# A second mixer whose scores use half of the matrix array each, and PSUM banks that are handed out in pairs

## The chip, the cores and the metric

The kernel runs on one core of one Trainium2 chip. A core has five engines that run side by side and wait for each other on counters: PE (TensorE, matrix products from SBUF into PSUM), DVE (VectorE), ACT (ScalarE), POOL (GpSimd) and SP, which issues transfers. Each engine works through its own list of instructions in the order in which the program gives them, so an instruction that waits holds up everything behind it on its engine. PSUM, into which PE writes, is used here as eight banks of 128 partitions by 512 fp32 numbers.

The metric is the device time of one execution in microseconds (us), the median over several runs.

## The reference: what is computed

Two layers on x of 256 tokens by 1024. Each layer is a half-weighted SwiGLU feed-forward part (hidden width 2816), a token mixer, and a second feed-forward part, all with RMSNorm in front and a residual around. The first layer's mixer is a gated DeltaNet; the second layer's mixer, which the change is about, is sliding-window attention:

```
proj = h @ w_in + b_in                      # 16 query heads, 4 key and value heads, 64 wide
s = einsum("bnqhgd,bnkhd->bnhgqk", q, kk) * 64**-0.5     # kk: this block of 128 keys and the one before
s = where(band of 128 keys, s, -inf)
p = softmax(concat([s, sink]))[..., :-1]
y = (p @ vv) @ w_out + b_out
```

There are two blocks of 128 tokens. Block 0 sees its own keys, block 1 sees its own and those of block 0.

## The kernel before, in words

Everything is resident in SBUF except the weights, which stream in once, 177 MB in all. Each 512 KB piece of weights (`raw`) is split in two fp32r parts: ACT rounds it to `whi` (line 296) and DVE subtracts to get `wlo` (line 297). A product then is two or three matrix products, such as `whi` by the high and low part of the activations side by side (line 348, 512 columns) and `wlo` by the high part (line 349, 256 columns).

**Feed-forward part** (`ffn`). After a first chunk that is done in another way, ten chunks of 256 hidden columns follow. A chunk makes four PSUM tiles, two of the gate (`pg`) and two of the up half (`pu`); each tile takes 16 matmuls, eight at line 348 and eight at line 349. Then the tile is emptied: ACT copies one half of it to SBUF (line 424 for a gate, 433 for an up tile) and DVE adds the other half to the copy (line 425 or 434). ACT's SiLU, POOL's product and the split of the result follow from SBUF. The down projection then accumulates in four or five `acc` tiles.

**Second mixer** (`swa`). The keys were written into `kz`, which holds each key head twice, in rows 0 to 63 for the one and rows 64 to 127 for the other head of a pair, with zeros elsewhere (POOL writes the zeros at line 1106). So one matmul with all 128 rows gives the scores of two query heads (`score`, line 1152): three of them for a pair of heads `j`, for block 1 against the older keys (`psp`) and for both blocks against their own (`psc`). DVE picks by mask (line 1162), adds the causal mask (1163) and takes the maximum (1166); ACT takes four exponentials out of PSUM (1176); POOL scales; PE transposes (`ppt`, 1186) and multiplies by the values (`po`, 1196).

**PSUM.** Two tags, `psA` and `psB`, have four buffers of one bank each. A new tile of a tag takes a buffer when everything that touched the tile in it is over.

**Order.** Nobody wrote the order of the engines' lists by hand, apart from a few `issue_after` edges. The framework collects the instructions and their dependences by tile, and a planner with an estimate of each duration orders every engine's list and hands out the buffers. So a change of the PSUM tiles may move instructions anywhere in the program.

Of the kernel before, what the change touches and what calls it, by code (L numbers as in the profile page):

```python
# [9 lines left out]
F32 = mybir.dt.float32  # L10
F32R = mybir.dt.float32r
AF = mybir.ActivationFunctionType
# [3 lines left out]
P = 128  # L16
D = 1024
T = 256
NT = T // P
# [9 lines left out]
BKV = 4  # L29
# [6 lines left out]
class Ticker:  # L36
    def __init__(self):
        self.active = []
# [167 lines left out]
class Kern:  # L206
    def __init__(self, ctx, tc):
        self.tc = tc
        self.nc = tc.nc
        self.cp = ctx.enter_context(tc.tile_pool(name="const", bufs=1))  # L210
        self.wp = ctx.enter_context(tc.tile_pool(name="wts", bufs=5))
        self.bp = ctx.enter_context(tc.tile_pool(name="big", bufs=11))
        self.sp = ctx.enter_context(tc.tile_pool(name="small", bufs=2))
        self.pp = ctx.enter_context(
            tc.tile_pool(name="ps", bufs=4, space=bass.MemoryType.PSUM)
        )
        self.consts()
        self.hold = None

# [881 lines left out]
    def swa(self, nrm, prep, w_in, w_out, after):  # L1101
        nc = self.nc
        bcol, bv, sk, bo = prep
        NP = BH // 2
        kz = self.big([P, BKV, 2, T], "kz")
        nc.gpsimd.memset(kz, 0.0)
        qT = self.big([P, NP, T], "qT")
        v = self.c2([P, NT, BKV * HD], "v")
        tk = Ticker()
# [18 lines left out]
        for f in range(2):  # L1128
            ps = self.psA("pk")
            self.proj_T(ps[:, :T], w, f, nrm)  # L1130
            for i in range(2):
                src = slice(64 * i, 64 * i + 64)
                for half in range(2):
                    dst = slice(64 * half, 64 * half + 64)
                    if half == i:
                        nc.scalar.activation(kz[dst, 2 * f + i, half, :], ps[src, :T], AF.Identity,
                                             bias=bcol[src, 8 + f:9 + f])
                    else:
                        nc.vector.tensor_scalar(kz[dst, 2 * f + i, half, :], ps[src, :T],
                                                bcol[src, 8 + f:9 + f], None, op0=ALU.add)  # L1140
        oT_h = self.big([P, KT, T], "oTh", F32R)
        oT_l = self.big([P, KT, T], "oTl", F32R)
# [1 line left out]
        def attend(j):  # L1144
            kv = j // 2
# [5 lines left out]
            def score(out, b, kt):  # L1151
                nc.tensor.matmul(out, lhsT=qT[:, j, b * P:(b + 1) * P], rhs=kz[:, kv, :, kt * P:(kt + 1) * P],  # L1152
                                 start=True, stop=True)
# [8 lines left out]
            nc.vector.copy_predicated(sc[:, 1], self.gt.bitcast(mybir.dt.int32).unsqueeze(1).to_broadcast([P, 2, P]), sp)  # L1162
# [11 lines left out]
            for b in range(NT):  # L1174
# [6 lines left out]
                out=pr, in0=pr, in1=l.unsqueeze(3).to_broadcast([P, NT, 2, P]), op=ALU.mult)  # L1181
            yield
            yield
            ps = self.psA("ppt")
            for n in range(4):
                nc.tensor.transpose(ps[:, n * P:(n + 1) * P], prv[:, n, :], self.ident)
            pv = ps.rearrange("p (b h q) -> p b h q", b=NT, h=2)
# [1 line left out]
            nc.vector.tensor_tensor(out=pT[:, 1:3], in0=pv[:, 1:2].to_broadcast([P, 2, 2, P]),  # L1189
                                    in1=self.M["st"].unsqueeze(2).to_broadcast([P, 2, 2, P]), op=ALU.mult)  # L1190
            yield
            po = self.psA("po")
            for b in range(NT):
                for i in range(2):
                    for kt in range(b + 1):
                        lastpo[0] = nc.tensor.matmul(po[64 * i:64 * i + 64, b * P:(b + 1) * P],  # L1196
                                         lhsT=v[:, kt, kv * HD:(kv + 1) * HD], rhs=pT[:, b + kt, i, :],
                                         start=kt == 0, stop=kt == b)
# [129 lines left out]
```

## Time and profile before

| | before |
|---|---|
| median of 3 runs (lowest, highest) | 1031.75 us (1031.38, 1031.99) |
| the profiled execution's own time | 1030.34 us |
| its span in the profile | 1028.6 us |
| PE busy | 1003.0 us, 98% of the span |
| DVE, ACT, POOL busy | 649.5, 552.5, 244.8 us |
| data moved | 177.05 MB, 172 GB/s on the mean |

A row of the timeline gives the start in us, the duration in us, engine, line, operation, output and inputs, shapes, and in square brackets how long the engine stood idle before and what ended that. A row of the windows view gives a stretch, its length, then for each engine the busy time and the number of instructions, then the granted clock of PE, the share of the transfer engines and GB/s. PE is drawn busy until a product has left its pipeline, so the starts of two matmuls that follow each other, and not their ends, tell how long one holds the array.

### The profile page before, as it was taken

To read this page: it belongs to the slowest core of one execution; us is meant where nothing else is said; L and a number is where in the kernel's file an instruction comes from. 1 tells how busy PE (TensorE), PEld (TensorE's weight loads), DVE (VectorE), ACT (ScalarE), POOL (GpSimd) and SP (SyncE) were. 2 spreads that over 40 slices of the span, in tenths; PEclk is the share of its full clock that TensorE was granted. 3 is DMA by queue.
4 is the path that set the end of the run, shared out by engine and by line. 5 is a ranking of instruction groups with operands and counts; after the bars stand their busy time and mean duration, and the time that the engine had idled before them with its cause. 6 is when DMAs were issued, how large, how long until landed. Compare 5 with 4: busy or idle time off the path is not lost.

```text
span 1028.6 us, 16500 instructions
## 1 busy us (share of the span) xinstructions
PE 1003.0 (98%) x6211; PEld 873.3 (85%) x6211; DVE 649.5 (63%) x967; ACT 552.5 (54%) x1007; POOL 244.8 (24%) x277
## 2 busy tenths in 40 slices
PE   8999999999979999999999999999999999999997
PEld 6888888899878888888888888888898678888886
DVE  6866654666896766666645666664567756666544
ACT  7556543457755646555434555554366645555432
POOL 2233610006744201322200032330021401323100
PEclk9999999999989999999999999999999999999999
DMA  7666666644443335666665666666653426666661
GB/s 250 202 190 186 192 198 196 187 149 127 129 150 90 122 104 164 194 187 193 198 192 182 189 200 187 184 204 193 203 188 120 136 90 205 195 188 192 200 189 42
DMA packets 135252, 177.05 MB, mean 172 GB/s; under 512 B 7186, under 2 KB 120196, under 8 KB 135172
## 3 DMA queue, kind: packets, MB, share of 16 engines
q1 hardware_dynamic: 131968, 171.46, 54.9%
q10 hardware_dynamic: 3204, 4.53, 1.5%
q8 instruction: 49, 0.80, 0.3%
q14 instruction: 31, 0.25, 0.1%
HBM read 174.92 MB, written 1.05 MB: 171 GB/s over the span
## 4 chain that ended last, share of the span: by engine, by line
PE 62%; issue 1%; DVE 1%; ACT 1%; POOLq 0%; POOL 0%; ACTq 0%
PE pg L348 11%; PE pu L348 11%; PE acc L343 7%; PE acc L341 7%; PE acc L342 7%; PE pu L349 6%; PE pg L349 6%; PE pgu L343 1%; PE pgu L342 1%; PE pgu L341 1%; PE pq L341 1%; PE pq L343 1%; PE pq L342 1%; PE psc L1152 1%; PE po L1196 1%
## 5 line engine op out<-in xcount | busy, mean ns | idle before, releaser
L297 DVE TENSOR_TENSOR wlo<-raw,whi 128x1024 fp32r<-128x1024 f32 x302 | 379.9, 1260 | 202.7 <-ACT whi L296 201.7
L296 ACT CAST whi<-raw 128x1024 fp32r<-128x1024 f32 x316 | 330.3, 1052 | 184.8 <-PE acc L343 84.2
L348 PE MATMUL pg<-hs,whi 128*128 128x512 f32 x640 | 225.6, 394 | 0.3 <-DVE hs L203 0.3
L348 PE MATMUL pu<-hs,whi 128*128 128x512 f32 x640 | 225.1, 393 | 0.0
L349 PE MATMUL pu<-hs,wlo 128*128 128x256 f32 x640 | 179.7, 281 | 0.3 <-DVE wlo L297 0.3
L349 PE MATMUL pg<-hs,wlo 128*128 128x256 f32 x640 | 178.9, 280 | 0.0
L348 PEld LDWEIGHTS pg<-hs,whi 128*128 128x128 f32 x640 | 119.9, 187 | 27.7 <-DVE hs L203 0.7
L348 PEld LDWEIGHTS pu<-hs,whi 128*128 128x128 f32 x640 | 119.8, 187 | 27.0
L435 POOL TENSOR_TENSOR act<-act,gate 128x256 f32<-128x256 f32 x80 | 60.2, 752 | 346.5 <-DVE act L434 337.7
L342 PE MATMUL acc<-wlo,ah 128*128 128x512 f32 (+1 forms) x340 | 128.4, 378 | 0.0
L343 PE MATMUL acc<-whi,al 128*128 128x512 f32 (+1 forms) x340 | 128.2, 377 | 0.0
L341 PE MATMUL acc<-whi,ah 128*128 128x512 f32 (+1 forms) x340 | 127.8, 378 | 0.0
L349 PEld LDWEIGHTS pu<-hs,wlo 128*128 128x128 f32 x640 | 120.9, 189 | 0.6 <-DVE wlo L297 0.6
L349 PEld LDWEIGHTS pg<-hs,wlo 128*128 128x128 f32 x640 | 120.9, 189 | 0.4
L341 PEld LDWEIGHTS acc<-whi,ah 128*128 128x128 f32 x340 | 64.0, 188 | 12.0
L342 PEld LDWEIGHTS acc<-wlo,ah 128*128 128x128 f32 x340 | 64.0, 188 | 11.8
L343 PEld LDWEIGHTS acc<-whi,al 128*128 128x128 f32 x340 | 63.9, 188 | 11.9
L438 POOL TENSOR_SCALAR ah<-act 128x256 fp32r<-128x256 f32 x80 | 69.0, 862 | 6.8
L341 PE MATMUL pcv<-hs,whi 128*128 128x256 f32 x192 | 56.5, 294 | 5.9 <-DVE cv L883 5.9
L424 ACT COPY gate<-pg 128x256 f32<-128x256 f32 x80 | 29.5, 369 | 58.9 <-PE pg L349 58.9
L433 ACT COPY act<-pu 128x256 f32<-128x256 f32 x80 | 29.5, 369 | 55.9 <-PE pu L349 55.9
L94 POOL TENSOR_TENSOR rst<-var,mhalf 128x1 f32<-128x1 f32 x10 | 5.6, 557 | 213.7 <-DVE var L92 213.7
(340 smaller groups left out, 1555.7 us busy)
## 6 DMA issues: line engine op xcount, KB each, us to landing
raw<-in_ffn_w_gu_dram SPq DMA_DIRECT2D x160, 512.0 KB, 4.4
raw<-in_ffn_w_down_dram SPq DMA_DIRECT2D x88, 512.0 KB, 4.2
raw<-in_a_w_in_dram SPq DMA_DIRECT2D x32, 512.0 KB, 4.5
raw<-in_ffn_w_gu_dram SPq DMA_DIRECT2D x32, 256.0 KB, 4.7
raw<-in_b_w_in_dram SPq DMA_DIRECT2D x12, 512.0 KB, 4.9
raw<-in_a_w_out_dram SPq DMA_DIRECT2D x8, 512.0 KB, 3.7
raw<-in_b_w_out_dram SPq DMA_DIRECT2D x8, 512.0 KB, 3.7
nw<-in_ffn_norm_dram ACTq DMA_DIRECT2D x3, 512.0 KB, 4.3
```

Of the source, the lines that this page charges most:

```text
L296: nc.scalar.copy(hi, raw)
L297: (eng or nc.vector).tensor_tensor(out=lo, in0=raw, in1=hi.bitcast(F32), op=ALU.subtract)
L341: nc.tensor.matmul(out, lhsT=lh, rhs=rh, start=start, stop=False)
L342: nc.tensor.matmul(out, lhsT=lh, rhs=rl, start=False, stop=False)
L343: return nc.tensor.matmul(out, lhsT=ll, rhs=rh, start=False, stop=stop)
L348: nc.tensor.matmul(out, lhsT=lh, rhs=r2, start=start, stop=False)
L349: return nc.tensor.matmul(out[:, :T], lhsT=ll, rhs=rh, start=False, stop=stop)
L424: nc.scalar.copy(g, pg[:, T:])
L433: nc.scalar.copy(a, pu[:, T:])
L435: nc.gpsimd.tensor_tensor(out=a, in0=a, in1=gates[f], op=ALU.mult)
L438: ahead[2] = nc.gpsimd.tensor_scalar(oh, a, 1.0, None, op0=ALU.mult)
L1152: nc.tensor.matmul(out, lhsT=qT[:, j, b * P:(b + 1) * P], rhs=kz[:, kv, :, kt * P:(kt + 1) * P], start=True, stop=True)
```

## The change

Three things are edited. In `swa`, the keys `kk` are kept once per half of the partitions, without zeros, and the scores of each head of a pair are computed by matmuls over its own 64 rows: four in place of three for a pair of heads, two with 256 columns and two with 128. The two heads' results lie in two different banks, so a pair of banks is taken as one tile (`pair`, two buffers of two banks each). `psA` now hands out the two halves of such a pair in turn, for every user of `psA` in the whole kernel, the feed-forward parts and the first mixer among them. And `ppt` and `po` move from `psA` to `psB`.

```diff
+        self.half = None
...
+    def pair(self, name):
+        self.half = None
+        return self.pp.tile([P, 2, 512], F32, tag="psA", name=name, bufs=2)
+
     def psA(self, name):
-        return self.pp.tile([P, 512], F32, tag="psA", name=name)
+        if self.half is None:
+            pair = self.pair(name)
+            self.half = pair[:, 1]
+            return pair[:, 0]
+        half, self.half = self.half, None
+        return half
...
-        kz = self.big([P, BKV, 2, T], "kz")
-        nc.gpsimd.memset(kz, 0.0)
+        kk = self.big([P, BKV, T], "kk")
...
-                        nc.scalar.activation(kz[dst, 2 * f + i, half, :], ps[src, :T], AF.Identity,
+                        nc.scalar.activation(kk[dst, 2 * f + i, :], ps[src, :T], AF.Identity,
...
-            psc, psp = self.psB("psc"), self.psB("psp")
-            sc = psc.rearrange("p (b h k) -> p b h k", b=NT, h=2)
-            sp = psp[:, 0:256].rearrange("p (h k) -> p h k", h=2)
-            score(sp, 1, 0)
-            score(sc[:, 1], 1, 1)
-            score(sc[:, 0], 0, 0)
+            ps = self.pair("psc")
+            for c, b, n in ((128, 1, 2), (0, 0, 1)):
+                for i in range(2):
+                    hs = slice(64 * i, 64 * i + 64)
+                    nc.tensor.matmul(ps[:, i, c:c + n * P], lhsT=qT[hs, j, b * P:(b + 1) * P], rhs=kk[hs, kv, 0:n * P],
+                                     start=True, stop=True)
+            sc = ps.rearrange("p h (b k) -> p b h k", k=256)[:, :, :, 0:P]
...
-            ps = self.psA("ppt")
+            ps = self.psB("ppt")
...
-            po = self.psA("po")
+            po = self.psB("po")
```

**How the order moves.** In the changed program line numbers are up to 14 higher (348, 349, 296, 297, 424 and 425 are now 360, 361, 308, 309, 436 and 437). Numbers behind names tell buffers apart; both halves of a pair bear the name that the first one got.

PE in the middle of the first feed-forward part, the first matmul of each tile (the 15 others of a tile are left out), before:

```order
L348 MATMUL pg_632<-hs_88,whi_620 128x512
...
L348 MATMUL pg_653<-hs_88,whi_620 128x512 [waits DVE_49]
...
L348 MATMUL pu_686<-hs_88,whi_674 128x512 [waits DVE_49]
...
L348 MATMUL pu_709<-hs_88,whi_674 128x512 [waits DVE_49]
...
L348 MATMUL pg_744<-hs_88,whi_732 128x512 [waits DVE_49]
```

and of the change:

```order
L360 MATMUL pu_567<-hs_88,whi_555 128x512 [waits DVE_49]
...
L360 MATMUL pu_677<-hs_88,whi_665 128x512 [waits DVE_49]
...
L360 MATMUL pg_624<-hs_88,whi_612 128x512 [waits DVE_49]
...
L360 MATMUL pg_734<-hs_88,whi_722 128x512 [waits DVE_49]
...
L360 MATMUL pu_677<-hs_88,whi_665 128x512 [waits DVE_49]
```

Before, the two tiles of a gate follow each other and then the two of an up half. Now halves of two pairs alternate: second half of `pu_567`, first of `pu_677`, second of `pg_624`, first of `pg_734`, second of `pu_677`. The counter value that a first half waits for is, in the built program, that of the DVE add which empties the half written directly before it: `pg_734` takes over the two banks of `pg_624` and waits for the add on the second half of `pg_624`, the tile right ahead of it in PE's list. A second half waits for the add on the first half of its own pair. Before, `pg_744` takes over the bank of `pg_632`, the fourth tile before it.

ACT's and DVE's lists of the change around the same place, with the emptying of the second half of `pg_624` (`gate_661`):

```order
L308 CAST whi_728<-raw_730 128x1024 [waits DMAHW6_49,PE_49,Activation_49]
L308 CAST whi_775<-raw_777 128x1024 [waits DMAHW7_49,PE_49,Activation_49]
L436 COPY gate_661<-pg_624 128x256 [waits PE_49,Pool_49]
L445 COPY act_694<-pu_677 128x256 [waits Pool_49]
L438 ACTIVATE gate_661<-gate_661 128x256 [waits DVE_49]
```

```order
L309 TENSOR_TENSOR wlo_729<-raw_730,whi_728 128x1024 [waits DMAHW6_49,PE_49,Activation_49]
L309 TENSOR_TENSOR wlo_776<-raw_777,whi_775 128x1024 [waits DVE_49,DMAHW7_49,PE_49,Activation_49]
L437 TENSOR_TENSOR gate_661<-gate_661,pg_624 128x256 [waits Activation_49]
L446 TENSOR_TENSOR act_694<-act_694,pu_677 128x256 [waits DVE_49,Activation_49]
L451 TENSOR_TENSOR al_131<-act_694,ah_128 128x256 [waits Pool_49]
```

The rows ahead of the copy and of the add are as they were before: two casts ahead of the one, two subtractions ahead of the other. The second cast waits, by its PE count, for the last line-360 matmul of that very tile, whose `whi` buffer it overwrites.

PE at the scores of the second and third pair of heads, of the change:

```order
L1167 MATMUL psc_7764<-kk_7462,qT_7463 128x256 [waits DVE_49,PE_49,Activation_49]
L1167 MATMUL psc_7764<-kk_7462,qT_7463 128x256
L1167 MATMUL psc_7764<-kk_7462,qT_7463 128x128 x2
...
L1167 MATMUL psc_7832<-kk_7462,qT_7463 128x256 [waits Activation_49]
L1167 MATMUL psc_7832<-kk_7462,qT_7463 128x256
L1167 MATMUL psc_7832<-kk_7462,qT_7463 128x128 x2
```

Where three full-height matmuls stood for a pair of heads, four of 64 rows stand now, and `psc_7764` waits for the last exponential that reads the scores before it.

More of the change, by code (lines that the diff above doesn't have):

```diff
@@ L1135, in swa @@
                     if half == i:
-                        nc.scalar.activation(kz[dst, 2 * f + i, half, :], ps[src, :T], AF.Identity,
+                        nc.scalar.activation(kk[dst, 2 * f + i, :], ps[src, :T], AF.Identity,
                                              bias=bcol[src, 8 + f:9 + f])
                     else:
-                        nc.vector.tensor_scalar(kz[dst, 2 * f + i, half, :], ps[src, :T],
+                        nc.vector.tensor_scalar(kk[dst, 2 * f + i, :], ps[src, :T],
                                                 bcol[src, 8 + f:9 + f], None, op0=ALU.add)
@@ L1149, in attend @@
             prv = pr.rearrange("p b h k -> p (b h) k")
-            def score(out, b, kt):
-                nc.tensor.matmul(out, lhsT=qT[:, j, b * P:(b + 1) * P], rhs=kz[:, kv, :, kt * P:(kt + 1) * P],
-                                 start=True, stop=True)
-            psc, psp = self.psB("psc"), self.psB("psp")
-            sc = psc.rearrange("p (b h k) -> p b h k", b=NT, h=2)
-            sp = psp[:, 0:256].rearrange("p (h k) -> p h k", h=2)
-            score(sp, 1, 0)
-            score(sc[:, 1], 1, 1)
-            score(sc[:, 0], 0, 0)
-            nc.vector.copy_predicated(sc[:, 1], self.gt.bitcast(mybir.dt.int32).unsqueeze(1).to_broadcast([P, 2, P]), sp)
+            ps = self.pair("psc")
[5 more added lines that the diff above has]
+            sc = ps.rearrange("p h (b k) -> p b h k", k=256)[:, :, :, 0:P]
+            nc.vector.copy_predicated(sc[:, 1], self.gt.bitcast(mybir.dt.int32).unsqueeze(1).to_broadcast([P, 2, P]),
+                                      ps[:, :, P:2 * P])
             nc.vector.tensor_tensor(out=sc[:, 0], in0=sc[:, 0], in1=self.neg.unsqueeze(1).to_broadcast([P, 2, P]),
```

## The prediction

> **What bounds the kernel now.** I read the page's busy shares first, then its clock strip and the shares of the chain of waits.
>
> ```profile
> span 1028.6 us, 16500 instructions
> PE 1003.0 (98%) x6211; PEld 873.3 (85%) x6211; DVE 649.5 (63%) x967; ACT 552.5 (54%) x1007; POOL 244.8 (24%) x277
> PEclk9999999999989999999999999999999999999999
> PE 62%; issue 1%; DVE 1%; ACT 1%; POOLq 0%; POOL 0%; ACTq 0%
> ```
>
> PE is busy in 98% of the span, at full clock in all but one of forty slices; DVE (63%) and ACT (54%) have room, and the chain runs through PE. So whatever makes PE wait lengthens the end by its whole length. Next I read the timeline of the first feed-forward part around the end of a gate tile.
>
> ```profile
> 475.66 0.39 PE L348 MATMUL pg<-hs,whi 128*128 128x512 f32 x1
> 475.89 0.28 PE L349 MATMUL pg<-hs,wlo 128*128 128x256 f32 x1
> 476.01 0.39 PE L348 MATMUL pu<-hs,whi 128*128 128x512 f32 x1
> 476.13 1.05 ACT L296 CAST whi<-raw 128x1024 fp32r<-128x1024 f32 x1 [0.34 <-PE pg L348]
> ...
> 477.08 0.37 ACT L424 COPY gate<-pg 128x256 f32<-128x256 f32 x1
> 477.21 1.23 DVE L297 TENSOR_TENSOR wlo<-raw,whi 128x1024 fp32r<-128x1024 f32 x1 [0.16 <-ACT whi L296]
> ...
> 478.36 0.42 DVE L425 TENSOR_TENSOR gate<-gate,pg 128x256 f32<-128x256 f32 x1
> ```
>
> The gate tile's last matmul starts at 475.89 and the next tile has the array from 476.01, without a gap. The tile is empty only when the add ends, at 478.36 + 0.42 = 478.78, 2.77 us later. Nobody feels it: four buffers stand in a ring, and the next tile into that bank comes three tiles on. The windows view of two tiles gives their length:
>
> ```profile
> 470.46:476.01 5.55, 5.55 (x35) 4.89 (x34) 3.88 (x7) 3.14 (x5) 1.66 (x3) 1.00 0.64 195
> ```
>
> 5.55 us for two tiles, PE busy throughout, clock 1.00. Emptying (2.77) is as long as one tile (5.55 / 2 = 2.78), and has three tiles of cover.
>
> **Term 1, the pairs.** The edit turns four separate banks into two pairs, and the order of the changed program shows what that does: a pair's first half waits for the add on the second half of the pair whose banks it takes, which is the tile PE has just written (`pg_734` behind `pg_624`). A second half waits for the add on the first half of its own pair, one tile further back, although that lies in another bank: two tiles of cover there, so no cost. So the cover of every other tile falls from three tiles to none. In the built order such a wait on the tile directly ahead stands at 17 places in each of the four feed-forward parts, 68 in all; the program before has none in these loops.
>
> Its price: ACT's and DVE's rows ahead of copy and add are the same as before, and the last cast ahead of the copy still waits for that tile's last line-348 product. So the chain above applies: cast 1.05 (released 0.12 us after the slot 476.01), copy behind it, subtraction to 478.44, add to 478.78. For the step from a DVE result to PE's restart I take the nearest restart of this kind:
>
> ```profile
> 814.76 0.34 DVE oTl L1201
> 815.15 0.73 PE L343 MATMUL acc<-whi,oTl 128*128 128x512 f32 x2 [1.64 <-DVE oTl L1201]
> ```
>
> 0.05 us (815.15 less 815.10). A stall is 2.77 + 0.05 = 2.82 us; everything behind on PE stands too, since its list is strict. Bounds: nothing shorter than copy and add alone, 0.37 + 0.42 with hand-overs of 0.12 (476.01 to 476.13), 0.03 (cast end 477.18 to 477.21) and 0.05, together 1.0 us, if casts and subtractions ran early; nothing above 3.3 if a second cast of 1.05 is only half done when the tile ends. I take 2.82, since the queue order that gave it stands unchanged. **68 x 2.82 = 192 us.**
>
> **Term 2, the clock.** PE's granted clock is not constant once PE pauses. Slices of 3.41 us around three pauses, and matmuls inside a slow one:
>
> ```profile
> 273.55:276.96 3.41, 2.16 (x19) 1.95 (x17) 3.33 (x5) 0.57 (x2) 2.86 (x3) 1.00 0.11 16
> 276.96:280.38 3.42, 3.25 (x27) 3.26 (x28) 3.39 (x4) 3.42 (x9) 2.29 (x1) 1.00 0.86 296
> 290.62:294.03 3.41, 0.49 (x5) 0.28 (x3) 3.41 (x4) 0.00 (x0) 1.89 (x2) 0.99 0.23 61
> 294.03:297.44 3.41, 0.48 (x2) 0.51 (x3) 3.41 (x8) 0.42 (x1) 0.00 (x0) 0.50 0.87 291
> 355.47:358.88 3.41, 1.86 (x10) 1.25 (x9) 1.87 (x8) 2.17 (x12) 1.61 (x2) 1.00 1.04 350
> 358.88:362.30 3.42, 2.80 (x25) 2.57 (x24) 1.73 (x7) 1.50 (x8) 0.41 (x1) 1.00 0.28 97
> 812.85:816.26 3.41, 1.76 (x9) 0.68 (x7) 3.24 (x10) 2.83 (x11) 1.03 (x2) 1.00 0.87 285
> 816.26:819.68 3.42, 3.40 (x16) 2.77 (x17) 2.54 (x3) 1.67 (x4) 2.31 (x2) 0.50 0.90 270
> 297.31 0.42 PE L342 MATMUL pcv<-hs,whi 128*128 128x256 f32 x1
> 297.53 0.42 PE L343 MATMUL pcv<-hs,wlo 128*128 128x256 f32 x1
> ```
>
> The two drops to 0.50 lie on one grid of 3.413 us (812.85 - 290.62 = 153 steps), and so I cut the others. A slice with 1.76 us or less of PE work is followed by a whole slice at 0.50, one with 1.86 or 2.16 by full clock. At 0.50 matmuls of 256 columns follow each other every 0.22 us (297.31 to 297.53) where they take 0.12 at full clock (475.89 to 476.01). So with idle time above about 1.65 us in one slice the next one does half its work. A stall of 2.82 us can hide from that only if a grid line cuts it so that neither side exceeds 1.65, that is between 1.17 and 1.65 us into it: 0.48 of 3.41, 14% of placements. In 52% it lies with all its idle time plus a whole busy slice behind it, losing 3.41 / 2 = 1.71 us; in 34% the slow slice holds the stall's tail and loses about 1.4. Mean 0.52 x 1.71 + 0.34 x 1.41 = 1.37; the top is 1.71. Since stalls follow each other every two tiles, a slow slice makes the next tiles longer and moves the phase; I take 1.5. **68 x 1.5 = 102 us**, between 0 (no rule as I read it) and 116.
>
> The Trainium skill speaks against this term: "TensorE: Matmul & The Clock Gate", Part 1, has the clock fall after an idle window of about 3.4 us; by that rule no stall of 2.82 us costs clock and the sum would be about 1238. The trace disagrees once: 1.65 us of idle time in the slice from 812.85 were enough.
>
> **Term 3, ends of the feed-forward parts.** The first products of the down projection wait for casts that stand behind the last gate tile's emptying; by the same chain, 1.5 us in each of four parts (0 to 3): **+6** (0 to 12).
>
> **Term 4, the first mixer.** Its `pcv` tiles come out of `psA` too:
>
> ```profile
> L883 DVE SCALAR_TENSOR_TENSOR cv<-pcv,wc,cv 128x253 f32<-128x253 f32 (+2 forms) x72 | 32.5, 472 | 10.9 <-ACT cv L880 10.4
> L880 ACT ACTIVATE cv<-pcv,wc 128x256 f32<-128x256 f32 x24 | 11.2, 472 | 5.1 <-PE pcv L343 5.0
> ```
>
> Emptying takes one ACT and three DVE instructions, 4 x 0.47 = 1.9 us. In the new order six such waits have 0.2 to 1.7 us of PE work ahead; they fall short by some 4.2 us together, and by up to 18 with a cast and a subtraction ahead. **+6** (0 to 20).
>
> **Term 5, the second mixer.**
>
> ```profile
> 780.32 0.43 PE psp L1152 x2
> 780.75 0.86 PE psc L1152 x4
> 782.18 0.37 ACT L1176 ACTIVATE att<-psc,smx 128x128 f32<-128x128 f32 x1
> 783.23 0.37 ACT L1176 ACTIVATE att<-psc,smx 128x128 f32<-128x128 f32 x1
> 787.21 0.59 PE po L1196 x8
> 787.81 0.59 PE ppt L1186 x4
> L1106 POOL MEMSET kz<- x1: 1813/1813/1813, 744.3 to 744.3; 128x2048 f32 x1
> ```
>
> The chain of waits gives 0.43 us for each of three score products per pair of heads: 8 x 3 x 0.43 = 10.3 us in all. The columns are the same now (2 x 256 + 2 x 128 against 3 x 256), so the gain is 0 if two 64-row products go one after the other, and half, 5.2, if they overlap. The trace has no 64-row product; the nearest, 64-column `po`, takes 0.074 each (0.59 / 8) where full-size transposes take 0.15 (0.59 / 4) on fewer columns, which says that narrow products are not dearer. I take the middle, **-2.6**.
>
> The Trainium skill's "TensorEngine Tiling (Array Packing)", Key Properties, lets two 64-row tiles work at once but drains PE at a change of mode; by its full gain the sum would be 2.6 us lower. No run shown so far has such products.
>
> Against it, a score pair is held from its first product (780.32) to its last exponential (783.23 + 0.37), about 3.3 us, or 4.3 with a cast ahead, while 24 projection products of 0.12 (2.9 us) stand between. Four places, 0.5 to 2.8 us each: **+5** (0 to 11). The memset (1.81 us) leaves POOL, which is idle three quarters of the span, and its row names nobody who waited for it: 0. `ppt` and `po` in `psB` find as many buffers as before: 0.
>
> **Sum.** 192 + 102 + 6 + 6 + 2.4 = 308 us. On the profiled execution's own time, 1030.34 (span 1028.6), that is 1339; the median, 1031.75, is 0.14% higher, which gives **1340**.
>
> **The rivals.**
>
> *The clock stays up* (0.10). For it: slices with 1.55 us of idle time (355.47) kept full clock, and only two drops are seen. Against it: 812.85. It would be 1031.75 + 192 + 14 = 1238.
>
> *Casts run early* (0.04). With PE stopped, casts and subtractions of later pieces could be done, leaving copy and add: 68 x 1.0 = 68 us, and a stall of 1.0 us leaves every slice over 1.86 us of work, so no half clock: 1031.75 + 68 + 14 = 1114. Against it: the cast ahead of the copy needs that tile's own last products.
>
> *Two slow slices for each stall* (0.05). If a slow slice with part of a stall in it counts as idle again, a second one follows: 68 x 1.5 more, about 1440.
>
> *The stalls are not there, and the change is faster* (0.02). One mechanism: the wait of a pair's first half stands one add earlier than I read it, on the tile before the last. Then emptying (2.77) ends as that wait comes up (a tile, 2.78), and terms 1, 2 and 3 are near 0; what remains is the score gain. Place: line 360's first product of each second tile; it decides for faster as soon as the wait ends within the tile. 1031.75 - 5.2 to 1031.75, say 1029. Against it: the built order, where the add's own input is the tile directly ahead. Half of the first mixer's 6 us would already cancel it to no change (0.01).
>
> **How the numbers follow.** Forecast 0.78, rivals 0.10, 0.04, 0.05 and 0.03. The forecast's own range is 1310 to 1375: stalls of 2.5 to 3.2 us, 1.2 to 1.7 us of clock. The range reaches down to the rival with the full clock, since some stalls may keep it, and up past 1375 for stalls with more cast ahead: 1235 to 1395. What a measurement of this kernel can tell from no change is 0.2%: faster 0.02, within it 0.01, slower 0.97.
>
> **What would show it.** Term 1: in the changed profile, groups of line 360 with some 48 us of idle time per feed-forward part (17 x 2.82), ended by DVE at the adds of lines 437 and 446; DVE and ACT busy as before. Term 2: the clock strip at 7 to 9 in the feed-forward stretches (a slow slice of 3.4 in some 10 us), and line 360 longer on the mean than 394 ns:
>
> ```profile
> L348 PE MATMUL pg<-hs,whi 128*128 128x512 f32 x640 | 225.6, 394 | 0.3 <-DVE hs L203 0.3
> L341 PE MATMUL pcv<-hs,whi 128*128 128x256 f32 x192 | 56.5, 294 | 5.9 <-DVE cv L883 5.9
> ```
>
> Term 4: idle time ahead of `pcv` tiles, ended by the DVE work that is line 883 now, some 6 us more than the 5.9 of before and at most 20. Term 5: score products in under 10.3 us. Wrong is term 1 if that idle time is below 100 us in all, and term 2 if the clock stays at 1.0 while they are there.

## The result

| | before | the change |
|---|---|---|
| median (lowest, highest) | 1031.57 us (1029.40, 1031.99), 4 runs | 1384.94 us (1384.14, 1386.32), 4 runs |
| ratio, 95% interval | | 1.3436 (1.3412 to 1.3460) |
| span of the profiled execution | 1028.6 us | 1382.4 us |
| mean granted clock of PE over the span | 0.99 | 0.90 |

The change costs 353 us; forecast were 308 (1340 us, range 1235 to 1395). The page of the changed kernel, three of the rows that answer to those shown of before:

```profile
span 1382.4 us, 16515 instructions
PE 1134.0 (82%) x6227; PEld 959.4 (69%) x6227; DVE 650.2 (47%) x967; ACT 550.8 (40%) x1007; POOL 236.7 (17%) x276
PEclk8988889999889998888899988889999998888899
```

DVE and ACT do what they did before (650 and 551 us). PE is busy in 82% of the span instead of 98%. Its busy time has still grown by 131 us with no more work to do, and the clock strip shows most of the reason: eights in all four feed-forward parts. Line 360's `pg` products are drawn 462 ns long on the mean, where line 348's were 394.

The waits of PE, grouped by who waits for whom, with the total, the number and the longest:

```profile
PE pg L360 <- DVE gate L437: 49.2, 18, 4.1
PE pu L360 <- DVE gate L437: 47.9, 18, 2.9
PE pg L360 <- DVE act L446: 42.4, 16, 2.7
PE pu L360 <- DVE act L446: 42.4, 16, 2.7
PE pcv L353 <- DVE cv L895: 14.6, 6, 8.1
PE pt L821 <- DVE X L812: 5.3, 1, 5.3
PE pcv L353 <- DVE kbr L711: 4.9, 1, 4.9
PE poT L1034 <- DVE on L1027: 4.3, 1, 4.3
PE psc L1167 <- ACT att L1186: 4.1, 3, 2.7
```

The first four rows are the stalls of the forecast: 18 + 18 + 16 + 16 = 68 of them, 181.9 us, 2.68 us each. The same view of before has no such row; its longest is a `pcv` wait of 5.9 us. One stall in the timeline of the fourth feed-forward part:

```profile
1175.20 0.28 PE L361 MATMUL pg<-hs,wlo 128*128 128x256 f32 x1
1175.44 1.04 ACT L308 CAST whi<-raw 128x1024 fp32r<-128x1024 f32 x1 [0.35 <-PE pg L360]
...
1176.40 0.37 ACT L436 COPY gate<-pg 128x256 f32<-128x256 f32 x1
1176.52 1.23 DVE L309 TENSOR_TENSOR wlo<-raw,whi 128x1024 fp32r<-128x1024 f32 x1 [0.17 <-ACT whi L308]
...
1177.66 0.41 DVE L437 TENSOR_TENSOR gate<-gate,pg 128x256 f32<-128x256 f32 x1
...
1178.13 0.51 PE L360 MATMUL pg<-hs,whi 128*128 128x512 f32 x1 [2.65 <-DVE gate L437]
```

Cast, copy, subtraction, add, and then PE again, 0.06 us after the add's end (1177.66 + 0.41 = 1178.07): the chain of the prediction, link by link. The idle time in brackets starts where the product before is drawn to end, 1175.20 + 0.28 = 1175.48. The next product could have had the array 0.12 us after 1175.20, so PE really lost 1178.13 - 1175.32 = 2.81 us: each stall has 0.16 us more than its idle time, and the views count them as busy.

The windows view by stage, before and then the change (from the first line-348 or line-360 product on: feed-forward part, first mixer, feed-forward part, feed-forward part, second mixer, feed-forward part), where the first figure after a comma is PE's busy time:

```profile
25.75:197.90 172.15, 171.83 (x899) 146.34 (x900) 105.40 (x135) 88.79 (x134) 45.70 (x69) 1.00 0.65 193
197.90:374.50 176.60, 164.88 (x1634) 155.29 (x1633) 128.97 (x252) 108.30 (x278) 69.09 (x52) 0.98 0.39 120
374.50:561.80 187.30, 187.24 (x984) 160.44 (x983) 112.22 (x145) 94.70 (x142) 32.95 (x42) 1.00 0.64 191
561.80:747.00 185.20, 185.08 (x975) 158.40 (x973) 111.82 (x144) 95.17 (x143) 34.70 (x43) 1.00 0.63 191
747.00:833.60 86.60, 84.31 (x579) 71.80 (x579) 62.06 (x118) 50.97 (x139) 21.19 (x14) 0.98 0.45 140
833.60:1028.60 195.00, 188.83 (x1051) 163.99 (x1049) 113.20 (x154) 96.52 (x148) 33.48 (x43) 0.99 0.55 168
```

```profile
31.67:278.10 246.43, 198.56 (x902) 164.46 (x901) 100.83 (x131) 88.65 (x133) 42.47 (x68) 0.90 0.45 133
278.10:490.20 212.10, 176.98 (x1639) 165.70 (x1638) 125.23 (x252) 111.01 (x278) 65.78 (x52) 0.91 0.33 100
490.20:754.30 264.10, 215.85 (x979) 178.12 (x978) 113.38 (x144) 92.84 (x142) 32.83 (x42) 0.90 0.45 135
754.30:1015.20 260.90, 214.61 (x975) 177.22 (x973) 113.83 (x144) 93.61 (x143) 32.83 (x42) 0.90 0.45 136
1015.20:1110.00 94.80, 83.59 (x595) 70.38 (x595) 63.62 (x119) 50.77 (x139) 20.01 (x14) 0.96 0.39 128
1110.00:1382.40 272.40, 219.87 (x1051) 184.05 (x1049) 112.65 (x153) 95.63 (x148) 33.42 (x43) 0.90 0.39 120
```

Length less busy time is idle time. The four feed-forward parts take 304 us more (1043.8 against 739.7): 188 idle and 116 busy. The first mixer takes 35.5 more (23.4 idle, 12.1 busy), the second 8.2 (8.9 idle), and the start, up to the first such product, 5.9 (31.67 against 25.75). Together 354.

### The profile page after: what moved, and what is told of

Read it like the earlier page. It is cut to its first block, busy times and chain, and to the rows that moved or that the text cites. A ratio compares the mean times of both kernels' runs of the same rounds, so it can differ in the third digit from the quotient of the medians.

```text
span 1382.4 us, 16515 instructions
## 1 busy us (share of the span) xinstructions
PE 1134.0 (82%) x6227; PEld 959.4 (69%) x6227; DVE 650.2 (47%) x967; ACT 550.8 (40%) x1007; POOL 236.7 (17%) x276
## 3 DMA queue, kind: packets, MB, share of 16 engines
HBM read 174.92 MB, written 1.05 MB: 127 GB/s over the span
## 5 line engine op out<-in xcount | busy, mean ns | idle before, releaser
L360 PE MATMUL pg<-hs,whi 128*128 128x512 f32 x640 | 277.6, 462 | 91.6 <-DVE gate L437 49.2
L360 PE MATMUL pu<-hs,whi 128*128 128x512 f32 x624 | 268.8, 460 | 90.3 <-DVE gate L437 47.9
L360 PEld LDWEIGHTS pg<-hs,whi 128*128 128x128 f32 x640 | 143.8, 225 | 137.8 <-DVE gate L437 54.9
L360 PEld LDWEIGHTS pu<-hs,whi 128*128 128x128 f32 x624 | 139.1, 223 | 135.1 <-DVE gate L437 53.7
L361 PE MATMUL pg<-hs,wlo 128*128 128x256 f32 x640 | 201.5, 315 | 0.0
L361 PEld LDWEIGHTS pg<-hs,wlo 128*128 128x128 f32 x640 | 144.2, 225 | 0.5
L361 PEld LDWEIGHTS pu<-hs,wlo 128*128 128x128 f32 x624 | 140.0, 224 | 0.3
L451 DVE TENSOR_TENSOR al<-act,ah 128x256 fp32r<-128x256 f32 x80 | 37.2, 465 | 103.4 <-POOL ah L450 103.4
L438 ACT ACTIVATE gate<-gate 128x256 f32<-128x256 f32 x80 | 31.9, 418 | 66.1 <-DVE gate L437 66.0
L353 PEld LDWEIGHTS pcv<-hs,whi 128*128 128x128 f32 x176 | 37.0, 211 | 24.5 <-issue 15.0
```

The costliest lines, as they stand in the source:

```text
L353: nc.tensor.matmul(out, lhsT=lh, rhs=rh, start=start, stop=False)
L360: nc.tensor.matmul(out, lhsT=lh, rhs=r2, start=start, stop=False)
L361: return nc.tensor.matmul(out[:, :T], lhsT=ll, rhs=rh, start=False, stop=stop)
L438: ahead[0] = nc.scalar.activation(g, g, AF.Silu)
L451: nc.vector.tensor_sub(al[ff // 8][:, ff % 8, :], a, oh.bitcast(F32))
```

## The experiments

Two kernels to compare with stay the same throughout: before (1030.6 to 1031.6 us beside these runs) and the change (1384.9). Theory A is that of the prediction: a stall is the wait of one half of a pair for the add on the other half, and stalls slow the clock.

**Pairs without the new scores.** `psA` hands out halves of pairs as in the change; keys and scores stay as they were.

```diff
...
+    def pair(self, name):
+
+        self.half = None
+        return self.pp.tile([P, 2, 512], F32, tag="psA", name=name, bufs=2)
+
     def psA(self, name):
-        return self.pp.tile([P, 512], F32, tag="psA", name=name)
+
+        if self.half is None:
+            pair = self.pair(name)
...
-            ps = self.psA("ppt")
+            ps = self.psB("ppt")
...
-            po = self.psA("po")
+            po = self.psB("po")
```

> The kernel before, with psA handing out halves of two-bank pairs (ppt and po in psB, as in the change), but the scores as before: full height, kz with zeros, psc and psp in psB. Theory A (each stall is the wait of a half-pair for the add on the other half): the stalls need nothing of the new scores, so 68 stalls and the slow slices stand as in the change; about 1385 us, 1375 to 1395, with line 360 idle for some 182 us. Rival B (the new scores and keys moved the order of the whole program and that costs): most of the loss is gone, under 1150 us.

Measured: 1389.65 us, ratio 1.3486 (1.3456 to 1.3517), clock 0.90. The stalls are 68 again, 180.8 us together:

```profile
PE pu L360 <- DVE gate L437: 47.9, 18, 2.9
PE pg L360 <- DVE gate L437: 47.7, 18, 2.7
...
```

The whole loss is there without one new score product, so rival B is out. The change, which has the new scores besides, is 4.7 us faster than this kernel, with intervals that just overlap.

**Scores without pairs.** Each head of a pair gets a bank of its own as a tile of its own.

```diff
-            psc, psp = self.psB("psc"), self.psB("psp")
...
+            ps = [self.psB("psc") for _ in range(2)]
...
+                    nc.tensor.matmul(ps[i][:, c:c + n * P], lhsT=qT[hs, j, b * P:(b + 1) * P], rhs=kk[hs, kv, 0:n * P],
...
+            for i in range(2):
+                nc.vector.copy_predicated(sc[i][:, 1], self.gt.bitcast(mybir.dt.int32), ps[i][:, P:2 * P])
+                nc.vector.tensor_tensor(out=sc[i][:, 0], in0=sc[i][:, 0], in1=self.neg, op=ALU.add)
+                nc.vector.tensor_reduce(out=m[:, :, i], in_=sc[i], axis=AX.X, op=ALU.max)
```

> The kernel before with single banks, and only the scores changed: keys once per partition half, each head's scores by 64-row products, the two heads of a pair in two separate one-bank tiles of psB (mask, causal mask and maximum then take one DVE instruction per head). Theory A: in the changed kernel's trace two 64-row products start 5 ns apart and a pair of heads takes 0.65 us in place of 1.29, so 8 x 0.64 = 5.1 us leave PE and nothing is added: 1026.5 us, 1024 to 1030. Rival B: a loss stays, over 1040 us. Rival D (the gain is hidden behind the softmax chain on DVE and ACT): 1030 to 1034.

Measured: 1031.70 us, ratio 1.0016 (1.0005 to 1.0026): no loss worth the name, and no gain either. Theory A's 1026.5 was wrong here, and the time lies where rival D put it; the last runs ask why.

**Two single banks.** `psA` gets half the PSUM that the pairs have, but every tile has its own dependences.

```diff
-        return self.pp.tile([P, 512], F32, tag="psA", name=name)
+        return self.pp.tile([P, 512], F32, tag="psA", name=name, bufs=2)
```

(and `ppt` and `po` in `psB`.)

> The kernel before with psA at two single banks in place of four (ppt and po in psB), so half the PSUM of the pairs, but each tile with its own dependences. Theory A: a tile then waits for the add on the tile before the last; emptying takes 2.77 + 0.05 us, a tile 2.78, so at most 0.1 us per tile: feed-forward loops of 114 to 118 us each (198 in the change), clock 1.0 there; in all 1032 to 1070, with what the first mixer loses. Rival C (what counts is that a tile has two places to go instead of four): loops near 198 us each and over 1300 us in all.

Measured: 1078.25 us, ratio 1.0466 (1.0452 to 1.0479), 8 us above the end of theory A's range. Its windows of the second feed-forward part and the first mixer:

```profile
212.70:407.10 194.40, 171.88 (x1638) 161.25 (x1637) 126.96 (x252) 110.59 (x278) 67.73 (x52) 0.96 0.35 110
407.10:597.50 190.40, 190.34 (x979) 159.32 (x978) 111.36 (x144) 94.74 (x142) 33.83 (x42) 1.00 0.62 188
```

This feed-forward part costs 3 us more than before at clock 1.00, with 0.06 us idle, where the pairs cost 77; the two after it lose 4 each and the first one 13. Rival C falls for the feed-forward parts: two banks with dependences of their own beat four that are tied in pairs. The first mixer loses 18 us here (194.40 against 176.60), so there the number of places does count; that and the 13 us of the first feed-forward part, whose cause is not tested, are why the time is above the range.

**Whole pairs.** The changed kernel with both gate tiles of a chunk (and both up tiles) written before either is emptied.

```diff
-            for f in range(2):
-                pg = self.psA("pg")
-                self.proj_T2(pg, wg, f, nrm.h)
+            pgs = self.pair("pg")
+            for f in range(2):
+                self.proj_T2(pgs[:, f], wg, f, nrm.h)
+            for f in range(2):
+                pg = pgs[:, f]
...
```

> The changed kernel, but in the feed-forward parts a chunk's two gate tiles are taken as one pair: the matmuls of both halves come first, then both are emptied; the same for the up half. Theory A: no half is written while the other is being emptied, and a new pair has two tiles (5.55 us) of cover, more than emptying two tiles takes: no stalls in the four loops (114 us each), clock 1.0, and what stays is the change's loss elsewhere, first mixer +35, second +8, start +6: about 1081 us, 1070 to 1095. Rival C: the loops stay near 198 us.

Measured: 1086.16 us, ratio 1.0541 (1.0523 to 1.0559), 5 us above theory A's figure. The four feed-forward parts take 741.0 us together (739.7 before, 1043.8 in the change), at clock 1.00. The second of them, which takes 187.30 us before and 264.10 in the change:

```profile
418.70:607.00 188.30, 186.51 (x979) 159.44 (x978) 117.75 (x144) 93.76 (x142) 34.69 (x42) 1.00 0.61 190
```

So it isn't pairs as such: it is that a pair's next tile waits for the emptying of the half written just before it. Rival C is out here too.

**The chain, shortened twice.** First each subtraction of weights, then each cast as well, is ordered behind the emptying in whose shadow it fell; PE and its pairs stay as they are. In the second run, shown here, `after` holds the tile's copy and add; in the first it holds the add alone.

```diff
...
+                for ins in after[i]:
+                    behind.enter_context(self.tc.issue_after(ins.ins))
                 pieces.append(self.wpiece(src[:, 4 * i:4 * i + 4, :], 4, 256,
...
+            done.append((cp, add))
```

> The changed kernel with an issue edge that puts each subtraction of weights behind the add that empties the tile in whose shadow it fell; the cast stays ahead of the copy. Theory A: the chain after a tile is cast, copy, add: 0.12 + 0.95 to the copy, 0.37, 0.03, 0.42, 0.05 = 1.94 us in place of 2.7, so line 360's idle time falls from 182 to 132 us. Clock rule (a grid slice with over 1.65 us idle makes the next one slow): a stall of 1.94 us escapes when the grid cuts it between 0.29 and 1.65, 40 in 100, so about 60 in 100 stalls cost a slow slice, some 41 slow slices in the feed-forward parts where the change has about 60: 1385 - 50 - 45 = 1290 us, 1265 to 1310. Rival E (the clock follows the mean share of idle time, no threshold): clock cost 116 x 132 / 182 = 84, so 1303 us and the slow slices at 43 or more.

> As the run before, and the casts too stand behind the copy and the add. Theory A: the chain is copy and add alone, 0.12 + 0.37 + 0.03 + 0.42 + 0.05 = 0.99 us: 68 x 0.99 = 67 us of idle time at line 360. Clock rule: no stall of 0.99 us makes a slice with 1.65 us of idle time, so the clock stays at 1.0 in the loops: 1385 - 115 - 116 = 1154 us, 1140 to 1175. Rival E (no threshold): clock cost 116 x 67 / 182 = 43, so 1197 us.

Measured: 1281.72 us (ratio 1.2428, 1.2392 to 1.2464) and 1163.69 us (1.1283, 1.1251 to 1.1316). PE's waits in the first of the two, and then in the second:

```profile
PE pg L365 <- DVE gate L443: 32.2, 18, 1.8
PE pu L365 <- DVE gate L443: 32.1, 18, 1.8
PE pg L365 <- DVE act L453: 28.6, 16, 1.8
PE pu L365 <- DVE act L453: 28.6, 16, 1.8
```

```profile
PE pg L365 <- DVE gate L443: 21.1, 34, 1.0
PE pg L365 <- DVE act L453: 17.4, 18, 1.0
PE pu L365 <- DVE gate L443: 17.2, 18, 1.0
```

| | a stall, us | stalls together, us | slow slices in the feed-forward parts | these parts, us |
|---|---|---|---|---|
| before | none | 0 | 1.2 | 740 |
| the change | 2.68 | 182 | 61.7 | 1044 |
| subtraction behind the add | 1.79 | 122 | 33.8 | 944 |
| cast and subtraction behind | 0.96 | 52 | 0.3 | 821 |

A slow slice is 3.41 us at a granted clock of 0.5, counted from the clock records; the 1.2 of before lie at the very end, from 1024.5 us on. The last row has only 54 stalls in place of 68: 16 further waits last only 0.19 to 0.24 us and add 3.6 us, so the 67 us that I had forecast were not reached. Each stall is near the sum of what still stands in the chain (forecast 1.94 and 0.99), and the clock goes with the stall's length, not with the idle share: with 52 us of idle time left in stalls of 0.96 us there are no more slow slices than before, where rival E wanted 43 us of clock. For 1.79 us the rule gives some 41 slow slices and rival E 43, so that run alone would not decide. The first run had 33.8, and its 1282 us are nearer to the rule's 1290 than to rival E's 1303.

PE's busy time in these parts is 24 us above before in the last kernel, although its clock is full. Some 0.27 us for each of its 70 waits, 19 us, are the two ends of a wait: 0.16 us in which the product before it is still drawn, and 0.11 us by which the first product behind it is longer (0.51 against 0.40 us in the timeline above). The other 5 us stay unexplained. So not all of the 116 us by which the change's busy time grew there is the clock.

**Whole pairs in the first mixer too.**

```diff
+            pss = self.pair("pcv")
+            for f in range(2):
+                self.proj_T(pss[:, f, :T], w, f, nrm)
             for f in range(2):
                 ct = col0 // P + f
-                ps = self.psA("pcv")
-                self.proj_T(ps[:, :T], w, f, nrm)
+                ps = pss[:, f]
```

> The kernel with whole pairs in the feed-forward parts, and in the first mixer too: the two pcv tiles of a convolution step are written as one pair, and only then both are emptied. Theory A (the first mixer's +35 us come from halves of pcv pairs that wait for each other, idle time first and slow slices after it): idle time in the first mixer falls from 35 towards the 12 of before, its stage from 214 to 177 to 190, and the whole to 1050 to 1065 us. Rival F (they come from having two places in place of four, as with two single banks, where that stage is 194 us with 22 idle): the stage stays at 194 or more and the whole at 1066 or more.

Measured: 1057.82 us, ratio 1.0259 (1.0235 to 1.0283). The window of the first mixer, with whole pairs in the feed-forward parts alone and with them here as well:

```profile
204.40:418.70 214.30, 179.12 (x1639) 167.87 (x1638) 125.23 (x252) 111.02 (x278) 65.70 (x52) 0.91 0.33 99
```

```profile
204.60:394.40 189.80, 170.56 (x1629) 159.77 (x1628) 126.98 (x250) 108.06 (x276) 65.68 (x52) 0.96 0.36 112
```

Of the 38 us that this stage had lost against before, 24.5 come back, 16 of them idle time, so rival F's 194 us do not hold. 13 stay. The other users of `psA` there (`pz`, `acc`) still take halves; they weren't tried.

**Where the score gain went.** Three runs. In the scores-only kernel each score product is issued twice:

```diff
-            for c, b, n in ((128, 1, 2), (0, 0, 1)):
+            for c, b, n in ((128, 1, 2), (0, 0, 1)) * 2:
```

> The kernel with only the scores changed, with every score product issued twice over the same place: some 3.4 to 5.1 us more work for PE in the second mixer (0.65 us for each of eight pairs of heads, less where the first pair of products costs a change of the array's mode anyway), nothing else. If the second mixer is bound by PE, 1035 to 1037 us. Rival D (the saved product time is hidden behind the softmax chain): within 1 us of the scores-only kernel, 1031 to 1033.

The kernel before, with full-height scores, gets the DVE work per head of the scores-only kernel:

```diff
+            for i in range(2):
+                nc.vector.copy_predicated(sc[:, 1, i], self.gt.bitcast(mybir.dt.int32), sp[:, i])
+                nc.vector.tensor_tensor(out=sc[:, 0, i], in0=sc[:, 0, i], in1=self.neg, op=ALU.add)
+                nc.vector.tensor_reduce(out=m[:, :, i], in_=sc[:, :, i], axis=AX.X, op=ALU.max)
```

> The kernel before, with full-height scores as they were and only the DVE work per head as in the scores-only kernel: three instructions on 128 or 256 columns for each head in place of three for both, 0.31 us more per pair of heads. If these instructions ate the gain of the 64-row products, this kernel is slower than before by about that gain, 3 to 5 us: 1034 to 1036. If they are hidden, 1030 to 1032.

And a layout that needs neither halves nor a split: PSUM is handed out anew at the head of the second mixer, as two banks for `psA`, two for `psB` and two pairs, and again behind it, as four single banks per tag.

```diff
+        self.banks("ps2", 2)
...
-        acc = [[ps("acc") for n in range(2)] for ps in (self.psA, self.psB)]
+        two = self.pair("acc")
+        acc = [[self.psA("acc") for n in range(2)], [two[:, n] for n in range(2)]]
...
+            K.banks("ps3", 4)
```

> The second mixer gets a PSUM layout of its own (two pairs of banks for scores, two single banks each for psA and psB; the second block's acc tiles lie in a pair), and everything else keeps four single banks per tag as before. Scores as in the change: 64-row products into a pair, mask, causal mask and maximum in one DVE instruction for both heads. Theory A: no stall in the feed-forward parts or the first mixer (stages 172, 177, 187, 185 and 195 us as before); the 64-row products save 3.4 us of PE in the second mixer and DVE has no extra instructions: 1030.6 - 3.4 = 1027 us, up to 1030 if the change of layout holds PE up at its two borders. Rival D (a score pair that is held until its last exponential stalls PE here as in the change, 4.7 us): 1032 to 1036.

Measured, all against before: doubled scores 1037.34 us (1.0064, 1.0047 to 1.0082), split DVE work 1032.88 (1.0021, 1.0008 to 1.0033), own banks 1045.30 (1.0146, 1.0125 to 1.0167). The second mixer's windows in the scores-only kernel, with split DVE work alone, with doubled scores and with its own banks (before: 86.60 long, 84.31 busy, clock 0.98):

```profile
746.00:832.50 86.50, 81.72 (x594) 68.35 (x595) 63.16 (x142) 50.47 (x139) 21.25 (x14) 0.98 0.43 141
```

```profile
749.50:838.40 88.90, 83.40 (x579) 70.59 (x579) 64.67 (x142) 50.79 (x139) 20.20 (x14) 1.00 0.43 137
```

```profile
747.90:840.60 92.70, 87.97 (x658) 74.44 (x659) 63.73 (x142) 50.92 (x139) 19.27 (x14) 0.98 0.41 131
```

```profile
747.40:839.90 92.50, 83.65 (x592) 70.27 (x592) 62.13 (x118) 50.73 (x139) 21.79 (x14) 0.94 0.41 131
```

Doubling costs its full price, 6.2 us in the stage (92.70 less 86.50) and 5.6 in the time, so more score work is not hidden, which speaks against rival D in its plain form. The split DVE work costs 2.3 us in the stage (88.90 less 86.60), and the 64-row products bring 2.4 back (88.90 to 86.50): that would be the balance of the scores-only kernel. But it is read from one profile each, and the one with split DVE work has no slow slice in this stage where the two others have one, so both figures may be up to 1.7 us too small. In the whole time split DVE work alone costs 2.2 us, between the two ranges named ahead of that run. The gain over it is 1.2 us by the medians and 0.5 by the ratios, with intervals of about 1.2 us on either side, so the size of the gain stays open.

The trace shows one more reason why the gain is small. Most sets of eight 64-row products (one pair of heads, two passes each) stand alone between products of another shape. One of them, between full-height `pq` products of the scores-only kernel:

```profile
774.68 0.28 PE L343 MATMUL pq<-hs,wlo 128*128 128x256 f32 x1
774.89 0.92 PE L1154 MATMUL psc<-kk,qT 64*128 64x256 f32 x8
775.74 0.39 PE L341 MATMUL pq<-hs,whi 128*128 128x256 f32 x1
...
```

The next `pq` product starts at 775.97. One `pq` product behind another takes 0.12 us, but the one ahead of the set holds the array for 0.21 us and the one behind it for 0.23. Within the set, the first two products (they start 6 ns apart, as all pairs do) take 0.10 us longer than the second two, and the last two 0.10 longer than the two before them. So the set costs 774.68 to 775.97 less two usual `pq` products, 1.29 - 0.24 = 1.05 us, of which 0.65 are the products themselves. The same stretch of before, three full-height products between `pq` products, takes 1.30. Such a set gains 0.25 us, and not the 0.64 on which theory A's 5.1 us rested: about 0.4 us go to changing over between the two kinds of product. Beside `po` products, which use 64 columns of the array, before pays for such changes too (0.20 us in place of 0.12 ahead of its scores), so not every pair of heads gains as little; PE's busy time in the stage falls by 2.6 us (84.31 to 81.72) for all eight.

Own banks did not do it either: 1045.30 us is beyond both forecasts. Of the 15 us lost, 5.9 lie in the second mixer (92.50 against 86.60) and 8.7 in the feed-forward part behind it (203.7 against 195.0). Its wait rows from 740 to 860 us name the borders of the layout, not the scores:

```profile
PE psT L107 <- DVE xn L96: 8.8, 3, 4.6
PE po L1203 <- DVE oTl L1208: 2.1, 2, 1.7
PE pgu L350 <- DVE hs L111: 1.4, 1, 1.4
PE pv L350 <- DVE hs L111: 1.4, 1, 1.4
```

The first, third and fourth rows stand at the norms ahead of the mixer and behind it, where before has no such wait; that the change of layout is their cause is argued from their place, not tested. Score pairs were not waited for, so rival D's other form (a pair held until its last exponential) isn't seen with two pairs for scores alone; in the change it is (4.1 us, last row of its waits). No kernel here beats before. Both heads' scores in one bank, which would need no pair, weren't tried.

## Why the prediction was right, and where it was off

The range held the time, the sign and the mechanism were right, and the likeliest case's own range (up to 1375) was missed by 10 us. Of the 45 us that the sum lacks, 4 lie in the four feed-forward parts, 29.5 in the first mixer, 5.8 in the second and 5.9 at the start. That 1385 still lies under 1395 is partly luck: I had put the top of the range there for stalls with more cast ahead, which did not occur.

- **Term 1, the stalls (192 forecast, 182 of idle time measured).** 68 was the exact number. The 2.68 us of idle time and the 2.82 forecast are counted from different points: 2.82 from the moment at which the next product could have had the array, 2.68 from the drawn end of the product before, 0.16 us later. Counted alike they are 2.84 and 2.82 us, 193 and 192 together. That they come from halves of a pair is shown by pairs alone and whole pairs; that cast and subtraction make up two thirds is shown by taking them out (1.79, 0.96). The rival with early casts needed what the last of these kernels does by its order, and its estimate of 1.0 us for copy and add was right for it. The rival without stalls is out with the first of the 68.
- **Term 2, the clock (102 forecast, about 98 by subtraction).** The feed-forward parts have 60 slow slices more than before; at 1.71 us each at most, 103 us. PE's busy time there grew by 116. Of that, 11 are the 0.16 us at the head of each stall (term 1), and 7 come from first products that are drawn 0.11 us longer; 98 are left for the clock, 1.44 us per stall, where I had 1.5. There were 0.9 slow slices per stall. I had seen only two drops in the profile of before; its clock records have a third, at 1024.5 us, behind waits at the end of the kernel. Rivals "the clock stays up" and "two slow slices for each stall" are both out (61.7 for 68).
- **Term 3, ends of the feed-forward parts (6 forecast, 4.2 measured).** `acc` waits for casts come to 4.8 us in all, 0.6 of them in the first mixer. Right.
- **Term 4, the first mixer (6 forecast, 35.5 measured).** This is the step that failed. I added up how far six waits fall short at their place in the order, 4.2 us, and stopped. The `pcv` waits alone grew from 5.9 to 14.6 + 4.9 us; two waits on tiles of `psB` (`pt` and `poT`) grew too, from 0.9 and 1.5 to 5.3 and 4.3; and the stage's slow slices went from 2 to 11, which I had left out altogether. My upper bound of 20 was too low for that. Pairs are shown to cause most of it (24.5 of 38 us come back with whole pairs); two single banks cost this stage 18 us, so fewer places may be part of the rest, which is not separated.
- **Term 5, the second mixer (2.4 forecast, 8.2 measured).** Two pairs of heads take 16 products from 1073.41 to the next `po` at 1074.91 where six of before (three per pair of heads, two passes each) take 780.15 to 781.45:

```profile
1073.41 1.58 PE L1167 MATMUL psc<-kk,qT 64*128 64x256 f32 x16 [0.69 <-ACT att L1186]
1074.91 0.33 PE L1206 MATMUL po<-att,v 128*64 128x128 f32 x2
```

```profile
780.15 0.60 PE L1152 MATMUL psp<-kz,qT 128*128 128x256 f32 x2
780.59 1.02 PE L1152 MATMUL psc<-kz,qT 128*128 128x256 f32 x4
781.45 0.59 PE L1152 MATMUL psp<-kz,qT 128*128 128x256 f32 x2
```

  That is 0.75 us against 1.30 per pair of heads: the two heads' products do run together, and in the trace they start 6 to 7 ns apart. "TensorEngine Tiling (Array Packing)" of the Trainium skill (Overview) gives up to twice the speed, which the trace nearly bears out, 1.7 times. But these 16 products are two pairs of heads in a row, and the six others stand alone in PE's list, where the changeover of about 0.4 us for a set takes much of the gain (under "Where the score gain went"). The prediction's middle, 2.6, was luck in its reason: I had read the 64-column products of line 1196 only as "not dearer", on more columns than the transposes, although both have 128, and in the trace of before they already mostly start 6 to 14 ns apart in twos. In the change the waits that I had priced at 5 came to 8.9 us, and busy time fell by 0.7 only, in place of 2.6, with two slow slices in the stage for one. Against pairs alone, with full-height scores, this stage is 3.6 us shorter (94.8 against 98.4), one slow slice fewer among them.
- **The start (nothing forecast, 5.9 measured).** PE had a clock of 0.78 up to the first line-360 product, against 1.00. In every kernel whose `psA` is handed out in halves the start took 31 to 32 us, in the others 26 to 28. The order of PE's first products had changed; why is not tested.

## What to carry to other kernels

A buffer that is handed out in pieces is waited for as a whole if dependences are kept per tile: before a tile is cut, ask which tile's last reader the next writer will now wait for, and how much work lies between. Write all pieces of such a tile before any is emptied, or give each piece a tile of its own; fewer buffers with dependences of their own can be far better than more that are tied together. And where a change makes short stalls everywhere, price each stage by its waits and its clock, not only the one with the largest number.

## What the runs showed of the hardware

The clock follows fixed slices of 3.413 us by how much PE did in each, in both directions. Counted from the clock records and PE's busy time over all twelve kernels, a slice at full clock was followed by a slow one 229 times and by a full one over 3,400 times. Those before a slow one had PE busy 0 to 1.93 us, but for two, and those before a full one 1.42 us or more, so the bound lies somewhere between 1.4 and 1.9 us. The two others had 2.4 us (whole pairs in the first mixer too, from 318.5 us on) and 2.2 us (doubled scores, from 313.1 us on); both are full of short products of the first mixer, 81 and 68 in one slice. A slow slice was followed by a full one 225 times, and only with PE busy 2.88 us or more, one and a half times to twice as much. That would fit if work counts and not busy time, which no run here separates. With less than 2.88 it was always followed by another slow one (58 slow slices were followed by a slow one, seven of them with more). That a slow slice lasts until PE is nearly fully busy in it I had not expected: the start of the change has four of them in a row, with short waits in the first three, behind one pause of 2.7 us.

Two 64-row products over different halves of the rows run at once: they start 6 to 7 ns apart, and inside a run of them a pair of heads takes 0.65 us against 1.30 for full-height products. A change from full-height products to these and back costs about 0.4 us, as worked out above.

"TensorE: Matmul & The Clock Gate" of the Trainium skill (Part 1) has the clock fall after an idle window of about 3.4 us. The length of the slice agrees; that it must be idle does not, since the slice from 812.85 of before, with 1.76 us of work, was followed by a slow one. The same page of the Trainium skill has a section "A second HAM failure mode: psum-queue depth-cycling" (HAM is its name for what sets the clock) that tells of short idle times between groups of products that make the clock swing. That agrees with the change (61.7 slow slices), with a bound from these runs: stalls of 0.96 us, at most one every two tiles, left the clock at 1.0.
